# Mixer group 0 in a fixed TensorE order: chunk scan and gate columns placed by hand instead of by the scheduler

## The chip, the cores and the metric

The kernel runs on one core of one Trainium2 chip. The metric is the device time of one execution in microseconds (us). Before the change it is 1347.84 us, the median of 3 runs (1347.83 to 1347.86).

## The reference

A two-layer decoder trunk over 512 tokens of width 1024, all in float32. Layer 0 is a Mamba-2 mixer and a convolutional feed-forward block; layer 1 is differential attention on shared keys and values and another such block. Only the mixer matters here:

```python
zxbcdt = rms_norm(x, ln_g) @ in_w                      # z (gate), x, B, C, dt
xbc = silu(causal_dwconv(xbc, conv_w, conv_b))
y = ssd_chunked(xs32 * dt, a, bm, cm)                  # 4 groups of 8 heads, 4 chunks of 128 tokens
    cb     = einsum('bclgn,bcsgn->bcgls', cc, bc)
    y_diag = einsum('bcgls,bgrcls,bcsgrp->bclgrp', cb, decay_in, xc)
    states = einsum('bclgn,bgrcl,bclgrp->bcgrpn', bc, decay_states, xc)   # carried from chunk to chunk
    y_off  = einsum('bclgn,bcgrpn,bgrcl->bclgrp', cc, states_in, exp(a_cs))
y = (y + xs32 * d_skip) * silu(z)
return rms_norm(y, per group) @ out_w
```

## The kernel before, in words

**Tiling.** The stream lies feature-major as eight tiles of 128 features by 512 tokens, each split into a high part `xgh` and a low part `xgl`. A weight block of 1024 by 128 columns is fetched by SyncE (SP) into a raw tile `wr`, split by ScalarE into `wh` (line 147) and by VectorE into `wl` (line 151), and multiplied in three passes per 128 features (lines 197, 198, 199): 24 matmuls of 128x512 per block, called **wide** below. Blocks are named after their column block: `in32` and `in36` are B and C of group 0, `in16` to `in19` its x, `in0` to `in3` its gate z; `in33`, `in37`, `in20` to `in23` the same of group 1.

**Groups and chunks.** The mixer goes over four groups. `conv_block` makes B, C and the four x blocks of a group: VectorE scales the product by the token norm (line 532, `u`), ScalarE starts the convolution (line 535, `ctmp`), VectorE adds three taps (line 537), ScalarE applies SiLU (line 539). Then the scan runs over four chunks of 128 tokens, called a, b, c and d in the code (`c0` to `c3` of a tile's number), while the gate columns fill TensorE.

**The steps of a chunk.** `turned` transposes B (tile `bt`). `decays` masks the decay matrix `m` on GpSimd (line 635) and takes eight exponentials on ScalarE (line 640). `masked` computes `cb` (line 646) and multiplies `m` by it on VectorE (line 647). `tokens` transposes x (`xs`, line 655) and weights it twice on VectorE (`xe`, `xd`, lines 658 and 660). `states` computes the chunk's state (`st`, line 685) and adds it to the one before (`S`). `preceding` applies the state before it (`yo`, line 676; VectorE, line 678). `products` are sixteen small matmuls (`y`, line 699 before and 701 after the change), and `outputs` adds them to x on VectorE (lines 708 and 711 before, 710 and 713 after). After the scan the group's x is gated (line 831), squared (`gsq`, line 833), summed (`gacc`, line 838), transposed to token norms (`tr_g`, line 448), taken to the power -1/2 by a chain of tiny VectorE steps ending in line 251, and spread back along the tokens by TensorE (`al_g`, line 458).

**What sets the order.** A scheduler places each engine's instructions at build time; within an engine they then run in that order. In groups 1 to 3 `woven` switches the scheduler off for TensorE (`manual_schedule`): after each of the 32 steps of `z_steps` (three wide matmuls each) a table `at` says which chunk steps come. Group 0 is left to the scheduler: `weave(scan(cs), z_blocks(g, zs), 2, 3)` offers the chunk steps in order and two gate blocks for every three of them. `tc.issue_after(x)` holds the placing of what follows until `x` has been placed. Small products share a ring of four banks of the matmul accumulator (`aux_bank`), so a small matmul also waits until the reader of an earlier one in its bank is done.

**Function tables.** Exponentials and SiLU lie in different tables of ScalarE; a change between them shows in the trace as ACT_TABLE_LOAD.

Of the kernel before, what the change touches and what calls it, by code (L numbers as in the profile page):

```python
# [18 lines left out]
P = 128  # L19
T = 512  # L20
D = 1024
KB = D // P
NT = T // P
# [3 lines left out]
HPG = 8  # L27
# [12 lines left out]
def trunk_kernel(ctx: ExitStack, tc, x, ssm_ln_g, ssm_in_w, ssm_conv_w, ssm_conv_b, ssm_dt_bias,  # L40
# [4 lines left out]
    act, dve, pool, pe, sync = nc.scalar, nc.vector, nc.gpsimd, nc.tensor, nc.sync  # L45
# [11 lines left out]
    def mm_bank(name):  # L57
        return pp.tile([P, T], F32, tag="mm", name=name)
# [129 lines left out]
    def chunk(key):  # L188
        while state["next"] <= state["use"] + AHEAD and state["next"] < len(plan):
            emit_chunk()  # L190
        state["use"] += 1
        k, h, l = ready.pop(0)
        assert k == key, (k, key)
        return h, l
# [59 lines left out]
    with tc.tile_pool(name="ph0", bufs=1) as p0:  # L254
# [24 lines left out]
        ps = aux_bank("pst")  # L279
# [193 lines left out]
    def weave(main, fill, num, den):  # L473

        owed = 0
        for _ in main:
            owed += num
            while owed >= den:
                owed -= den
                next(fill, None)  # L480
        run(fill)
# [37 lines left out]
    with tc.tile_pool(name="ssm_y", bufs=1) as yp, tc.tile_pool(name="ssm", bufs=1) as sp:  # L519
        def in_block(key):  # L520
            wh, wl = chunk(key)
            if key in ("in32", "in36"):
                return ps_b0 if key == "in32" else ps_b1
            ps = mm_bank("ps_" + key)
            for k in range(KB):
                state["last"] = mm3(ps, wh[:, k, :], wl[:, k, :], xgh[k], xgl[k], k == 0, k == KB - 1)
            return ps
# [81 lines left out]
        class Chunk:  # L609
# [22 lines left out]
            def decays(self):  # L632


                pool.affine_select(out=self.m, in_=self.m, pattern=[[0, HPG], [1, P]], compare_op=ALU.is_ge,
                                   fill=NEG, base=0, channel_multiplier=-1)
                for h in range(HPG):
                    v = self.m[:, 4 * (h % 2) + h // 2, :]
                    col = self.hh.start + h
                    act.activation(v, v, AF.Exp, bias=ncum[:, col:col + 1])  # L640

            def masked(self):

                cs = self.cs
                ps = aux_bank("cb" + self.tag)
                pe.matmul(ps[:, :P], self.bT[:, cs], self.cT[:, cs], start=True, stop=True)
                dve.tensor_tensor(out=self.m, in0=self.m, in1=ps[:, :P].unsqueeze(1).to_broadcast([P, HPG, P]),
                                  op=ALU.mult)

            def tokens(self):  # L650

# [28 lines left out]
            def states(self):  # L680

                tag, c = self.tag, self.c
                if c < NT - 1:
                    ps = aux_bank("st" + tag)
                    pe.matmul(ps, self.bt, fl(self.xe), start=True, stop=True)
                    self.S = sp.tile([P, HPG, 64], F32, tag="S", name="S" + tag, bufs=2)
                    if c == 0:
                        act.activation(fl(self.S), ps, AF.Copy)
                    else:
                        dve.tensor_tensor(out=self.S, in0=self.prev.S, in1=self.per_head(et), op=ALU.mult)  # L690
                        dve.tensor_tensor(out=self.S, in0=byh(ps), in1=self.S, op=ALU.add)

            def products(self):

# [27 lines left out]
                    add_to_stream(m, ps, 16, norm)  # L722
                    yield

        def z_blocks(g, zs):
            for b in range(4):
                ps = in_block("in%d" % (4 * g + b))
                z = sp.tile([P, T], F32, tag="z", name="z%d_%d" % (g, b), bufs=4)
                dve.tensor_tensor(out=z, in0=ps, in1=rr[0], op=ALU.mult)
                act.activation(z, z, AF.Silu)  # L730
                zs.append(z)
                yield

        def z_steps(g, zs):
            for b in range(4):
                wh, wl = chunk("in%d" % (4 * g + b))
                ps = mm_bank("ps_in%d" % (4 * g + b))
                for k in range(KB):
                    state["last"] = mm3(ps, wh[:, k, :], wl[:, k, :], xgh[k], xgl[k], k == 0, k == KB - 1)
                    if k == KB - 1:  # L740
                        z = sp.tile([P, T], F32, tag="z", name="z%d_%d" % (g, b), bufs=4)
                        dve.tensor_tensor(out=z, in0=ps, in1=rr[0], op=ALU.mult)
                        act.activation(z, z, AF.Silu)
                        zs.append(z)
                    yield

# [3 lines left out]
                cs.append(Chunk(g, c, bT, cT, xs, cs[-1] if cs else None))  # L750
            return cs

        def scan(cs):
            for t in range(NT + 1):
                if t < NT:
                    cs[t].tokens()
                    if t < NT - 1:
                        cs[t].turned()
                    cs[t].masked()
                if t == 0:  # L760
                    cs[2].decays()
                    cs[3].decays()
                if t:
                    cs[t - 1].preceding()
                    cs[t - 1].states()
                    cs[t - 1].products()
                    cs[t - 1].outputs()
                yield

        def woven(cs, g, zs):  # L770

            def pair(a, b):
                a.products()
                b.products()
                a.outputs()
                b.outputs()

            a, b, c, d = cs
            at = {0: (a.turned, b.turned, c.decays), 1: (a.masked, b.masked, d.decays),
                  10: (a.tokens,), 11: (b.tokens,), 13: (a.states,), 15: (b.preceding, b.states),  # L780
                  16: (lambda: pair(a, b), c.turned, c.masked), 18: (c.tokens,), 19: (c.preceding, d.tokens),
                  20: (d.masked,), 21: (c.states,), 24: (d.preceding,), 25: (lambda: pair(c, d),)}
            with tc.manual_schedule(engines={mybir.EngineType.PE}):
                behind = 5 if g == 1 else 0
                for n, _ in enumerate(z_steps(g, zs)):
                    for f in at.get(n - behind, ()):
                        f()

# [17 lines left out]
        for g in range(NG):  # L806
            bT = sp.tile([P, T], F32, tag="bT", name="bT%d" % g, bufs=2)
            cT = sp.tile([P, T], F32, tag="cT", name="cT%d" % g, bufs=2)
            xs_ = sp.tile([P, 4, T], F32, tag="xs", name="xs%d" % g, bufs=2)
            cs = chunks(g, bT, cT, xs_)  # L810
            for c in cs:
                c.fetch()
            conv_block(16 + g, "in%d" % (32 + g), bT)
            if g:
                prev = normed(*todo)
            conv_block(20 + g, "in%d" % (36 + g), cT)
            if g == 0:
                params_a()
            xs = [xs_[:, b, :] for b in range(4)]
            for b in range(4):  # L820
                if b >= 2:
                    cs[b - 2].decays()
                conv_block(4 * g + b, "in%d" % (16 + 4 * g + b), xs[b])
            zs = []
            if g:
                woven(cs, g, zs)
            else:
                weave(scan(cs), z_blocks(g, zs), 2, 3)
            acc = None
            for b in range(4):  # L830
                dve.tensor_tensor(out=xs[b], in0=xs[b], in1=zs[b], op=ALU.mult)
                sq = sp.tile([P, T], F32, tag="gsq", name="gsq%d_%d" % (g, b), bufs=2)
                act.activation(sq, xs[b], AF.Square)
                if b == 0:
                    acc = sq
                else:
                    a2 = sp.tile([P, T], F32, tag="gacc", name="gacc%d_%d" % (g, b), bufs=2)
                    (pool if b == 1 and g else dve).tensor_tensor(out=a2, in0=acc, in1=sq, op=ALU.add)
                    acc = a2
            factor = lambda: token_rsqrt(acc, sp, "g%d" % g, 512)  # L840
            if g == 0:
                params_b()
                todo = g, xs, factor()
            elif g < NG - 1:
                run(out_proj(g - 1, *prev, None))
                todo = g, xs, factor()
            else:
                op = out_proj(g - 1, *prev, None)
                for _ in range(3):
                    next(op)  # L850
                rt = factor()
                for _ in range(2):
                    next(op)
                prev = normed(g, xs, rt)
                run(op)
# [486 lines left out]
```

## Time and profile before

| What | us |
|---|---|
| median of 3 runs | 1347.84 |
| the profiled execution | 1347.89 |
| its span from the first to the last instruction | 1346.2 |
| TensorE (PE) busy in the span | 1340.2 |
| VectorE (DVE), ScalarE (ACT), GpSimd (POOL) busy | 913.8, 644.1, 105.0 |
| group 0's gate blocks, chunks, and blocks in33 and in37 | 50.88 to 98.09 |

The profiled execution is 0.05 us above the median, so a sum made against it can be carried to the median with that difference. The span leaves out 1.7 us that lie around it. A row of the timeline gives start, duration, engine, line, operation, tiles and count, and at the end in brackets how long the engine had been idle and what released it. Matmuls overlap, so the cost of one in a row of them is the distance from its start to the next start, not its printed duration. The chain of work that ended last lists pieces with just that cost.

### The profile page before, as it was taken

Reading aid. Unit: us, or ns where it says so; the run is one execution under the profiler, and the core shown is the slowest. Engines: PE = TensorE matmul, PEld = TensorE weight load, DVE = VectorE, ACT = ScalarE, POOL = GpSimd, SP = SyncE. Lnnn points to the kernel's source line nnn. Section 1 sums busy time; section 2 is a strip of 40 time slices with the busy share of each in tenths; the row PEclk is TensorE's granted clock in tenths of the full one; section 3 lists DMA queues with packets and bytes.
Section 4 is the critical chain, followed back from the end, with each engine's and each line's share of the span. In section 5 each row is a group of like instructions: output and inputs, shape, how many; then the busy total and the mean of one; then the engine's idle time right before and its main releaser. Section 6 shows DMA issues by size and latency. Waiting matters only on the chain.

```text
span 1346.2 us, 16887 instructions
## 1 busy us (share of the span) xinstructions
PE 1340.2 (100%) x6423; PEld 1097.1 (81%) x6423; DVE 913.8 (68%) x1527; ACT 644.1 (48%) x1058; POOL 105.0 (8%) x141
## 2 busy tenths in 40 slices
PE   9999999999999999999999999999999999999998
PEld 7878888888888888888888887777888888888887
DVE  5989788788877774367754556778777773367743
ACT  6696553652444442234433556777654442134420
POOL 6330401200110000000002200000100000000000
PEclk9999999999999999999999999999999999999999
DMA  7543533432333332333323422221233322333322
GB/s 205 160 150 94 145 98 111 132 94 71 94 94 94 97 107 94 94 94 95 101 79 105 131 79 93 69 81 50 64 94 94 94 94 95 95 105 97 94 94 78
DMA packets 179825, 134.98 MB, mean 100 GB/s; under 512 B 6492, under 2 KB 163552, under 8 KB 179744
## 3 DMA queue, kind: packets, MB, share of 16 engines
q1 hardware_dynamic: 173872, 120.73, 29.6%
q0 software_dynamic: 4592, 12.08, 3.0%
q8 instruction: 50, 0.82, 0.3%
q10 hardware_dynamic: 1280, 1.10, 0.2%
q14 instruction: 31, 0.25, 0.1%
HBM read 131.64 MB, written 2.25 MB: 99 GB/s over the span
## 4 chain that ended last, share of the span: by engine, by line
PE 97%; DVE 1%; ACT 1%; DMA 0%; issue 0%; SPq 0%
PE ps_g L198 6%; PE ps_u L199 6%; PE ps_g L199 6%; PE ps_u L197 6%; PE ps_u L198 6%; PE ps_g L197 6%; PE ps_in L197 5%; PE ps_in L199 5%; PE ps_in L198 5%; PE ps_d L198 3%; PE ps_d L199 3%; PE ps_d L197 3%; PE ps_d L923 3%; PE ps_d L921 3%; PE ps_d L922 3%; PE ps_o L198 2%
## 5 line engine op out<-in xcount | busy, mean ns | idle before, releaser
L197 PE MATMUL ps_u<-xgh,wh_u 128*128 128x512 f32 x352 | 137.4, 390 | 0.0
L198 PE MATMUL ps_g<-xgl,wh_g 128*128 128x512 f32 x352 | 137.1, 389 | 0.0
L197 PE MATMUL ps_g<-xgh,wh_g 128*128 128x512 f32 x352 | 137.0, 389 | 0.0
L199 PE MATMUL ps_u<-xgh,wl_u 128*128 128x512 f32 x352 | 137.0, 389 | 0.0
L199 PE MATMUL ps_g<-xgh,wl_g 128*128 128x512 f32 x352 | 137.0, 389 | 0.0
L198 PE MATMUL ps_u<-xgl,wh_u 128*128 128x512 f32 x352 | 136.9, 389 | 0.0
L197 PE MATMUL ps_in<-xgh,wh_in 128*128 128x512 f32 x304 | 126.0, 414 | 0.0
L151 DVE TENSOR_TENSOR wl_d<-wr_d,wh_d 128x1024 fp32r<-128x1024 f32 (+1 forms) x46 | 54.2, 1179 | 96.9 <-ACT wh_d L147 96.7
L199 PE MATMUL ps_in<-xgh,wl_in 128*128 128x512 f32 x304 | 119.8, 394 | 0.0
L198 PE MATMUL ps_in<-xgl,wh_in 128*128 128x512 f32 x304 | 119.2, 392 | 0.0
L147 ACT ACTIVATE wh_d<-wr_d 128x1024 fp32r<-128x1024 f32 (+1 forms) x46 | 47.1, 1024 | 130.6 <-PE ps_d L923 58.0
L882 DVE TENSOR_TENSOR uu<-ps_u,nr_f 128x512 f32<-128x512 f32 x44 | 30.4, 691 | 77.6 <-PE ps_u L199 77.6
L953 ACT ACTIVATE hh<-vg 128x512 fp32r<-128x512 f32 x44 | 27.8, 632 | 114.9 <-DVE vg L952 114.9
L198 PEld LDWEIGHTS ps_g<-xgl,wh_g 128*128 128x128 f32 x352 | 66.1, 188 | 14.0 <-DVE xgl L430 0.3
L199 PEld LDWEIGHTS ps_u<-xgh,wl_u 128*128 128x128 f32 x352 | 66.1, 188 | 13.7
L197 PEld LDWEIGHTS ps_g<-xgh,wh_g 128*128 128x128 f32 x352 | 66.1, 188 | 13.7
L199 PEld LDWEIGHTS ps_g<-xgh,wl_g 128*128 128x128 f32 x352 | 66.1, 188 | 13.7
L198 PEld LDWEIGHTS ps_u<-xgl,wh_u 128*128 128x128 f32 x352 | 66.1, 188 | 13.6
L197 PEld LDWEIGHTS ps_u<-xgh,wh_u 128*128 128x128 f32 x352 | 66.1, 188 | 13.5
L147 ACT ACTIVATE wh_g<-wr_g 128x1024 fp32r<-128x1024 f32 x44 | 46.7, 1061 | 50.3 <-PE ps_u L198 30.9
L197 PE MATMUL ps_d<-hh,wh_d 128*128 128x512 f32 x176 | 68.5, 389 | 0.0
L198 PE MATMUL ps_d<-hl,wh_d 128*128 128x512 f32 x176 | 68.5, 389 | 0.0
(361 smaller groups left out, 3175.1 us busy)
## 6 DMA issues: line engine op xcount, KB each, us to landing
wr_g<-in_ffn_up_w_dram SPq DMA_DIRECT2D x44, 512.0 KB, 3.7
wr_u<-in_ffn_up_w_dram SPq DMA_DIRECT2D x44, 512.0 KB, 3.7
wr_d<-in_ffn_down_w_dram SPq DMA_DIRECT2D x42, 512.0 KB, 3.6
wr_in<-in_ssm_in_w_dram SPq DMA_DIRECT2D x40, 512.0 KB, 3.8
m<-cumd POOLq DMA_DIRECT2D x16, 512.0 KB, 4.7
wr_out<-in_ssm_out_w_dram SPq DMA_DIRECT2D x16, 512.0 KB, 3.3
wr_k<-in_kv_w_dram SPq DMA_DIRECT2D x8, 512.0 KB, 3.7
wr_q<-in_q_w_dram SPq DMA_DIRECT2D x8, 512.0 KB, 3.7
```

Of the source, the lines that this page charges most:

```text
L147: return act.activation(self.wh[:, :self.n], self.raw[:, :self.n], AF.Copy)
L151: return eng.tensor_tensor(out=self.wl[:, :self.n], in0=self.raw[:, :self.n], in1=self.wh[:, :self.n].bitcast(F32), op=ALU.subtract)
L197: pe.matmul(ps, wh, xh, start=start, stop=False)
L198: pe.matmul(ps, wh, xl, start=False, stop=False)
L199: return pe.matmul(ps, wl, xh, start=False, stop=stop).ins
L882: dve.tensor_tensor(out=u, in0=ps, in1=r, op=ALU.mult)
L921: pe.matmul(pss[b], hh[k][:, ts], wh[:, k - k0, :], start=k == 0, stop=False)
L922: pe.matmul(pss[b], hh[k][:, ts], wl[:, k - k0, :], start=False, stop=False)
L923: pe.matmul(pss[b], hl[k][:, ts], wh[:, k - k0, :], start=False, stop=k == stop)
L953: act.activation(h, ga, AF.Copy)
```

## The change

Group 0 now goes through `woven` too, with a table of its own; the scheduler no longer places its TensorE work. Against the table of the other groups, the exponentials of all four chunks stand at step 7, `cb` of chunks a and b stands behind the state of chunk a, `cb` of the third chunk one step behind the pair of products, and the end of the scan is spread to step 31. Four more edits belong to it: chunk b's `preceding` and `states` are placed after the weighing of its `m` (`taken_up`), the outputs of chunk a on VectorE after chunk b's new state (`behind`), the second gate block's SiLU after the exponentials of chunk d, and the weights fetched ahead at the third gate block after the exponentials of chunk b. The first state of group 0 is copied out by VectorE (line 688) instead of ScalarE.

```diff
                     self.S = sp.tile([P, HPG, 64], F32, tag="S", name="S" + tag, bufs=2)
-                    if c == 0:
+                    if c == 0 and self.g == 0:
+                        dve.tensor_copy(fl(self.S), ps)
+                    elif c == 0:
                         act.activation(fl(self.S), ps, AF.Copy)
                     else:
                         dve.tensor_tensor(out=self.S, in0=self.prev.S, in1=self.per_head(et), op=ALU.mult)
-                        dve.tensor_tensor(out=self.S, in0=byh(ps), in1=self.S, op=ALU.add)
+                        self.summed = dve.tensor_tensor(out=self.S, in0=byh(ps), in1=self.S, op=ALU.add).ins
...
-        def z_steps(g, zs):
+        def z_steps(g, zs, cs):
             for b in range(4):
-                wh, wl = chunk("in%d" % (4 * g + b))
+                key = "in%d" % (4 * g + b)
+                if g == 0 and b == 2:
+                    with tc.issue_after(cs[1].decayed):
+                        wh, wl = chunk(key)
+                else:
+                    wh, wl = chunk(key)
...
-                        act.activation(z, z, AF.Silu)
+                        if g == 0 and b == 1:
+                            with tc.issue_after(cs[3].decayed):
+                                act.activation(z, z, AF.Silu)
+                        else:
+                            act.activation(z, z, AF.Silu)
...
-            def pair(a, b):
+            def pair(a, b, behind=None):
                 a.products()
                 b.products()
-                a.outputs()
+                with tc.issue_after(behind) if behind is not None else nullcontext():
+                    a.outputs()
                 b.outputs()
 
+            def taken_up(c):
+                with tc.issue_after(c.weighed):
+                    c.preceding()
+                    c.states()
...
+            if g == 0:
+                at = {0: (a.turned, b.turned), 7: (a.decays, b.decays, c.decays, d.decays),
...
+                      17: (lambda: taken_up(b),), 20: (lambda: pair(a, b, b.summed), c.turned), 21: (c.masked,),
...
             for b in range(4):
-                if b >= 2:
+                if g and b >= 2:
                     cs[b - 2].decays()
                 conv_block(4 * g + b, "in%d" % (16 + 4 * g + b), xs[b])
             zs = []
-            if g:
-                woven(cs, g, zs)
-            else:
-                weave(scan(cs), z_blocks(g, zs), 2, 3)
+            woven(cs, g, zs)
```

What this makes of the engines' orders shows at three places. On TensorE before, the end of the scan stands inside the last gate block `in3` (tile `ps_in3`): transposes, `cb`, `yo`, one wide matmul, a state and the products of chunk c follow each other.

```order
L655 MATMUL xs0_3_839<-ident_77,xs0_429 128x128 x4
L646 MATMUL cb0_3_846<-cT0_428,bT0_427 128x128
L676 MATMUL yo0_2_849<-cT0_428,S0_1_788 128x128 x4
L198 MATMUL ps_in3_934<-xgl5_99,wh_in3_807 128x512
L685 MATMUL st0_2_855<-xe0_2_769,bt0_2_775 128x512
L699 MATMUL y0_2_860<-m0_2_437,xd0_2_771 64x128 x8
L199 MATMUL ps_in3_934<-xgh5_91,wl_in3_808 128x512
```

After, `cb` of chunk c, the transposes of c and the pieces behind them stand between whole steps of three wide matmuls, in the third gate block `in2` and the fourth.

```order
L646 MATMUL cb0_2_854<-cT0_428,bT0_427 128x128
L197 MATMUL ps_in2_793<-xgh6_92,wh_in2_641 128x512
L198 MATMUL ps_in2_793<-xgl6_100,wh_in2_641 128x512
L199 MATMUL ps_in2_793<-xgh6_92,wl_in2_642 128x512
L655 MATMUL xs0_2_860<-ident_77,xs0_429 128x128 x4
L197 MATMUL ps_in2_793<-xgh7_93,wh_in2_641 128x512
L198 MATMUL ps_in2_793<-xgl7_101,wh_in2_641 128x512
L199 MATMUL ps_in2_793<-xgh7_93,wl_in2_642 128x512
L676 MATMUL yo0_2_875<-cT0_428,S0_1_808 128x128 x4
L655 MATMUL xs0_3_881<-ident_77,xs0_429 128x128 x4
```

So the pieces moved one gate block earlier and no longer follow each other directly, except `yo` and the transposes behind it. On VectorE after, one step of chunk b's outputs stands ahead of chunk b's new state (`S_1`, line 693), the outputs of chunk a and the rest of chunk b's behind it, and then the weighing of chunk c's `m`.

```order
L678 TENSOR_TENSOR er_1_434<-yo_1_800,er_1_434 128x512
L692 TENSOR_TENSOR S_1_808<-S_0_773,dec 128x512
L710 TENSOR_SCALAR xs_429<-xs_429,c_103,y_1_829 128x128
L693 TENSOR_TENSOR S_1_808<-st_1_806,S_1_808 128x512
L710 TENSOR_SCALAR xs_429<-xs_429,c_103,y_0_820 128x128 x4
L710 TENSOR_SCALAR xs_429<-xs_429,c_103,y_1_829 128x128 x3
L647 TENSOR_TENSOR m_2_437<-m_2_437,cb_2_854 128x1024
```

Before, chunk a's outputs stood ahead of chunk b's state. On ScalarE after, at the start of group 1 (blocks `in23` and `in4`), exponentials of group 1's last chunk alternate with SiLU and convolution steps, so table loads stand between them.

```order
L418 ACTIVATE le<-le 128x2
L147 ACTIVATE wh_in_1187<-wr_in_1185 128x1024
L640 ACTIVATE m_3_1038<-m_3_1038,ncum 128x128
L539 ACT_TABLE_LOAD
L539 ACTIVATE cT_1024<-ctmp_1140 128x512
L535 ACTIVATE ctmp_1179<-u_1177,c_102 128x512
```

Before, that exponential stood ahead of the load that `bT` needs, and no load stood between `wh_in23` and `ctmp` of the next block.

More of the change, by code (lines that the diff above doesn't have):

```diff
@@ L639, in decays @@
                     col = self.hh.start + h
-                    act.activation(v, v, AF.Exp, bias=ncum[:, col:col + 1])
+                    self.decayed = act.activation(v, v, AF.Exp, bias=ncum[:, col:col + 1]).ins
             def masked(self):
@@ L646, in masked @@
                 pe.matmul(ps[:, :P], self.bT[:, cs], self.cT[:, cs], start=True, stop=True)
-                dve.tensor_tensor(out=self.m, in0=self.m, in1=ps[:, :P].unsqueeze(1).to_broadcast([P, HPG, P]),
-                                  op=ALU.mult)
+                self.weighed = dve.tensor_tensor(
+                    out=self.m, in0=self.m, in1=ps[:, :P].unsqueeze(1).to_broadcast([P, HPG, P]), op=ALU.mult).ins
             def tokens(self):
@@ L723, in out_proj @@
                     yield
-        def z_blocks(g, zs):
+        def z_steps(g, zs, cs):
             for b in range(4):
-                ps = in_block("in%d" % (4 * g + b))
-                z = sp.tile([P, T], F32, tag="z", name="z%d_%d" % (g, b), bufs=4)
-                dve.tensor_tensor(out=z, in0=ps, in1=rr[0], op=ALU.mult)
-                act.activation(z, z, AF.Silu)
-                zs.append(z)
-                yield
-        def z_steps(g, zs):
-            for b in range(4):
-                wh, wl = chunk("in%d" % (4 * g + b))
-                ps = mm_bank("ps_in%d" % (4 * g + b))
+                key = "in%d" % (4 * g + b)
[4 more added lines that the diff above has]
+                    wh, wl = chunk(key)
+                ps = mm_bank("ps_" + key)
                 for k in range(KB):
@@ L742, in z_steps @@
                         dve.tensor_tensor(out=z, in0=ps, in1=rr[0], op=ALU.mult)
-                        act.activation(z, z, AF.Silu)
+                        if g == 0 and b == 1:
[3 more added lines that the diff above has]
+                            act.activation(z, z, AF.Silu)
                         zs.append(z)
@@ L751, in chunks @@
             return cs
[L753 to L768, printed above, removed]
@@ L770, in woven @@
         def woven(cs, g, zs):
-            def pair(a, b):
+            def pair(a, b, behind=None):
                 a.products()
                 b.products()
-                a.outputs()
+                with tc.issue_after(behind) if behind is not None else nullcontext():
+                    a.outputs()
                 b.outputs()
+            def taken_up(c):
+                with tc.issue_after(c.weighed):
+                    c.preceding()
+                    c.states()
             a, b, c, d = cs
[L779 to L782, printed above, removed]
+            if g == 0:
+                at = {0: (a.turned, b.turned), 7: (a.decays, b.decays, c.decays, d.decays),
+                      11: (a.tokens,), 12: (b.tokens,), 14: (a.states,), 15: (a.masked, b.masked),
+                      17: (lambda: taken_up(b),), 20: (lambda: pair(a, b, b.summed), c.turned), 21: (c.masked,),
+                      22: (c.tokens,), 23: (c.preceding, d.tokens), 24: (d.masked,), 26: (c.states,),
+                      30: (d.preceding,), 31: (lambda: pair(c, d),)}
+            else:
+                at = {0: (a.turned, b.turned, c.decays), 1: (a.masked, b.masked, d.decays),
+                      10: (a.tokens,), 11: (b.tokens,), 13: (a.states,), 15: (b.preceding, b.states),
+                      16: (lambda: pair(a, b), c.turned, c.masked), 18: (c.tokens,), 19: (c.preceding, d.tokens),
+                      20: (d.masked,), 21: (c.states,), 24: (d.preceding,), 25: (lambda: pair(c, d),)}
@@ L783, in woven @@
             with tc.manual_schedule(engines={mybir.EngineType.PE}):
                 behind = 5 if g == 1 else 0
-                for n, _ in enumerate(z_steps(g, zs)):
+                for n, _ in enumerate(z_steps(g, zs, cs)):
                     for f in at.get(n - behind, ()):
```

## The prediction

> **What bounds the kernel now.** I read the page first: its totals and the shares of the chain that ended last.
>
> ```profile
> span 1346.2 us, 16887 instructions
> PE 1340.2 (100%) x6423; PEld 1097.1 (81%) x6423; DVE 913.8 (68%) x1527; ACT 644.1 (48%) x1058; POOL 105.0 (8%) x141
> PE 97%; DVE 1%; ACT 1%; DMA 0%; issue 0%; SPq 0%
> ```
>
> TensorE is busy for 1340.2 of 1346.2 us and carries 97% of the chain. The end moves only by what TensorE's stream gets shorter or by what it is made to wait. A busy TensorE can still lose time between matmuls, so I took the stretch that the change rewrites: from the first matmul of `in0` to the first of `in20`. It holds the same work before and after.
>
> ```profile
> 50.88:98.09 47.21, 47.16 (x273) 37.19 (x272) 38.42 (x67) 38.59 (x88) 22.09 (x28) 1.00 0.60 182
> ```
>
> The columns are the stretch's length, then the busy time of PE, PEld, DVE, ACT and POOL, then the granted clock, DMA share and GB/s. TensorE works through all 47.21 us at clock 1.00, with DVE and ACT at four fifths. Next the timeline, for the price of a wide matmul and for what lies around the products.
>
> ```profile
> 61.62 0.39 PE L197 MATMUL ps_in<-xgh,wh_in 128*128 128x512 f32 x1
> ...
> 71.38 0.39 PE L198 MATMUL ps_in<-xgl,wh_in 128*128 128x512 f32 x1
> 71.82 1.09 PE L699 MATMUL y<-m,xd 128*64 128x128 f32 x16
> 72.85 0.66 PE L655 MATMUL xs<-ident,xs 128*128 128x128 f32 x4
> ...
> 80.92 1.02 PE L685 MATMUL st<-xe,bt 128*128 128x512 f32 x2
> 81.87 1.09 PE L699 MATMUL y<-m,xd 128*64 128x128 f32 x16
> ```
>
> From 61.62 to 71.38 lie 43 starts, 0.227 us each. Six blocks of 24 make 144 wide matmuls or 32.69 us, so the chunk work costs 47.21 - 32.69 = 14.5 us now. That is all the change can touch directly. Part is loss: the products at 71.82 come 0.44 us after a wide start where 0.227 would do, and those at 81.87 come 0.95 us after their state.
>
> **What the fixed order costs on TensorE.** Groups 1 to 3 run such an order already, so the chain has the price of each piece, the slow restart of the wide stream behind it included. Columns: start, cost, piece.
>
> ```profile
> 125.97 0.44 PE cb L646 x4
> 132.58 0.44 PE xs L655 x4
> 135.55 0.86 PE st L685 x2
> 137.80 0.89 PE yo L676 x8
> 138.69 0.86 PE st L685 x2
> 140.26 1.90 PE y L699 x32
> 142.16 0.26 PE bt L666
> 87.86 0.30 PE pst L236 x2
> ```
>
> With the new order's pieces in turn: the first transposes with `ps_cum`, `pst` and two `bt`, about 0.55 in two pieces (estimated from the two transposes of parameters, 0.30, and one `bt`, 0.26); two `xs` 0.88; `st` 0.86; two `cb` 0.44; `yo` and `st` 1.75; two products and `bt` 1.90 + 0.10 lead-in + 0.23; single `cb` 0.23; `xs` 0.44; `yo` and `xs` 1.33; `cb` 0.23; `st` 0.86; `yo` 0.89; two products with two `pst` 2.25; two `pst` 0.28. That is 13.2 us: 1.3 us less than 14.5 if TensorE never waits. I take 1.2, since some of these prices are read to 0.03 us only.
>
> **The waits it adds.** First, `ps_cum` stands two wide matmuls earlier (at 51.56 on the clock of before) and needs the copy of `cum`.
>
> ```profile
> 51.32 0.28 DVE L596 COPY cum<-ps_dec 128x128 f32<-128x128 f32 x1
> 52.01 0.27 PE L602 MATMUL ps_cum<-ident,cum 128*128 128x128 f32 x1
> ```
>
> The copy ends at 51.60; with the hand-over TensorE waits about 0.15 us.
>
> Second, the third chunk's `cb` takes the bank of chunk b's state, so it waits for VectorE's addition (line 693). VectorE has put one step of chunk b's outputs ahead of that addition, and this step waits for the end of chunk b's products.
>
> ```profile
> 77.92 0.69 DVE L691 TENSOR_TENSOR S<-st,S 128x512 f32<-128x512 f32 x1
> 79.19 1.12 DVE L708 SCALAR_TENSOR_TENSOR xs<-xs,c,y 128x128 f32<-128x128 f32 x4 [0.58 <-PE y L699]
> 80.23 0.68 DVE L660 TENSOR_TENSOR xd<-xs,dt 128x512 f32<-128x512 f32 x1
> ...
> 78.05 1.09 PE L699 MATMUL y<-m,xd 128*64 128x128 f32 x16
> 79.08 0.66 PE L655 MATMUL xs<-ident,xs 128*128 128x128 f32 x4
> ```
>
> Outputs start 0.11 us after TensorE has gone on (79.08 to 79.19) and cost 0.26 each (79.19 to 80.23, four). So the addition ends 0.11 + 0.26 + 0.69 = 1.06 us after, about 1.15 with the hand-over. TensorE meanwhile has `bt` (0.14 to the next start) and three wide matmuls with a slow restart (0.77), 0.91 us. Wait: 0.25 us. Behind it the third chunk's transposes need the bank of chunk a's products, that is four more outputs: the addition's slot of 0.60 and 4 x 0.26, done at about 2.2; TensorE arrives at 2.1. Wait: 0.10 us. Queued behind both on TensorE is everything, so they count in full. The other chunk steps have cover: the first state, whose copy the change moves to VectorE (taken as one line 660 step, 0.60), is multiplied at 62.7 and copied by about 64.2, and `yo` of chunk b, behind 54 wide matmuls and 2.9 us of pieces, comes at 66.0. Were that 1.8 us of cover gone, TensorE would wait for the rest.
>
> Third, the exponentials. They must be done before the products of chunks a and b. TensorE reaches those behind 63 wide matmuls (14.3 us) and 4.6 us of pieces, at 69.8, chunk b's 1.0 later.
>
> ```profile
> 61.58 6.70 POOL L635 TENSOR_SCALAR_AFFINE_SELECT m<-m 128x1024 f32<-128x1024 f32 x4
> 66.60 1.28 ACT L640 ACT_TABLE_LOAD   x1
> 67.90 9.48 ACT L640 ACTIVATE m<-m,ncum 128x128 f32<-128x128 f32 x32
> ```
>
> GpSimd's masks do not move; the first ends near 63.2 (6.70 / 4 behind 61.58). ScalarE before starts its exponentials only at 67.90, behind two SiLUs. After, one SiLU and a load stand ahead and it starts at 63.3. Chunk b's are done 16 x 0.296 = 4.7 us later at 68.0, its weighing (1.2 us) at 69.3. TensorE wants it at 70.8. No wait, 1.5 us of cover.
>
> **What is late next.** ScalarE changes table ten times instead of six between 58 and 109 us, and the group norm hangs on it.
>
> ```profile
> 96.94 1.14 ACT L833 ACTIVATE gsq<-xs 128x512 f32<-128x512 f32 x2
> 97.98 0.80 ACT L535 ACTIVATE ctmp<-u,c 128x512 f32<-128x512 f32 x1
> 98.68 1.05 ACT L147 ACTIVATE wh_in<-wr_in 128x1024 fp32r<-128x1024 f32 x1
> 99.63 0.80 ACT L535 ACTIVATE ctmp<-u,c 128x512 f32<-128x512 f32 x1
> ...
> 103.18 1.28 ACT L539 ACT_TABLE_LOAD   x1
> 104.47 0.63 ACT L539 ACTIVATE bT<-ctmp 128x512 f32<-128x512 f32 x1
> 98.91 0.68 DVE L838 TENSOR_TENSOR gacc<-gacc,gsq 128x512 f32<-128x512 f32 x1
> 99.92 0.60 PE L448 MATMUL tr_g<-ident,gacc 128*128 128x128 f32 x4
> 110.82 0.60 PE L458 MATMUL al_g<-ident,tr_g 128*128 128x128 f32 x4
> ```
>
> If `in20` starts 0.7 us earlier, at 97.4, `tr_g` behind 18 of its wide matmuls (8 before) is reached at 97.4 + 4.1 = 101.5. VectorE's sum `gacc` was done at 99.6 before; adding VectorE's steps in the new order from the end of `in33` (ten of 0.60, one split of about 1.1, three taps of about 0.7) I get 101.4. A tie. `al_g` behind 4 wide matmuls of `in22` is reached at 97.4 + 48 x 0.227 + 0.44 + 4 x 0.227 = 109.65. Ahead of the last step of line 251 on VectorE now stands a tap of block `in20`, which needs ScalarE's start of that block. ScalarE is free for `wh_in22` when TensorE has read `in37`, at 97.5, and then has two splits of 0.95, two squares 1.04, two starts (0.71 and 0.80), five exponentials 1.5, three loads with what follows at 1.29 each 3.9, two SiLUs of 0.54, and 0.4 of small steps: 11.3 us, to 108.8. With the tap and line 251 the norm is there at 109.7. I take a wait of 0.1 us there; each later ScalarE step counts in full.
>
> Two views of a table change differ. In the row, the next instruction starts 1.29 us after a load of 1.28 (103.18 to 104.47). The Trainium skill (ScalarE: Activation LUTs, What ACT_TABLE_LOAD costs) adds to a load of about 1283 ns a drain of about 1380 ns, 2.66 us per change; the trace agrees with the load and shows no drain. By it the three changes would put ScalarE 3 x 1.38 = 4.1 us later, an estimate from that page.
>
> **Sum.** 1.2 us less work, 0.15 + 0.25 + 0.10 + 0.10 = 0.6 us of waits: 0.6 us gained. 1347.89 - 0.6 = 1347.3 for the profiled execution, 1347.25 for the median, which lies 0.05 below it; I say 1347.3. Beyond 110 us the orders converge and TensorE has no wait to win back. Bounds: no waits at all gives 1346.6 and is the low end. At the high end one more step the size of a load (1.29) late at `al_g` gives 1348.6.
>
> **The rivals.** *Full gain* (0.12): the ties fall well and VectorE is quicker; 1347.84 - 1.2 = 1346.6. For it: the same pieces in group 1 show no wait. Against: the wait for line 693 is built into the order.
>
> *ScalarE late at the norm* (0.16), the one on the other side: from the point at which ScalarE's start of `in20` comes more than 0.6 us after 108.8, `al_g` eats the gain. The masks of group 1's third chunk are the likely cause, since their fetch now waits for products that come about 5 us later; one load's worth gives 1347.3 + 1.3 = 1348.6. For it: both norm steps tie in my sum. Against: nothing in ScalarE's rows shows a reserve spent.
>
> *A table change costs a second load's time* (0.02): three times 1.28 at `al_g`, 1347.3 + 3.8 = 1351.1. Against: the rows above. The drain in the Trainium skill's page is such a price.
>
> *Nothing moves* (0.05): VectorE's waits grow to the whole 1.2; 1347.84.
>
> The forecast keeps 0.65: 1346.9 to 1347.8. The range 1346.6 to 1348.6 leaves out the double load and part of the tails. I call a difference over 0.2%, 2.7 us, faster or slower, about what a measurement of this kernel can tell from no change. The stretch cannot give 2.7 us, so faster gets 0.02. Slower needs 3.3 us of waits: 0.04. Within: 0.94.
>
> **What would show it.** Right: `in20` starts near 97.4 instead of 98.09; `cb` of chunk c stands about 0.25 us behind its wide neighbour; exponentials from about 63.3 to 72.8; `al_g` near 109.8. Wrong: `in20` at or after 98.09 (my prices or waits), a start of `tr_g` or `al_g` more than 0.7 us behind its neighbour (the ScalarE rival), products that wait for the weighing, or any difference that lies after 130 us.

## The result, and the profile after

The changed kernel takes 1350.13 us (median of 20 runs, 1349.20 to 1350.95) against 1347.99 us (median of 20 runs, 1347.66 to 1348.48) for the kernel before: 2.1 us slower, a ratio of 1.0016 with a 95% interval of 1.0010 to 1.0022. That is under the 0.2% that I had set as the bound for slower, and outside the predicted range of 1346.6 to 1348.6. The profiled execution of the changed kernel took 1350.06 us. From its page, the totals and the shares of the chain that ended last:

```profile
span 1348.4 us, 16893 instructions
PE 1340.5 (99%) x6423; PEld 1097.3 (81%) x6423; DVE 915.6 (68%) x1528; ACT 651.3 (48%) x1063; POOL 103.6 (8%) x141
PE 95%; DVE 1%; ACT 1%; DMA 1%; issue 0%; POOL 0%; SPq 0%; POOLq 0%
```

The same work on TensorE, now 2.2 us longer: TensorE waits. The stretch from `in0` to `in20`, and the waits of TensorE from 45 to 125 us (total, times, longest):

```profile
50.66:97.83 47.17, 46.87 (x274) 37.14 (x272) 38.45 (x66) 40.05 (x86) 19.39 (x27) 1.00 0.64 183
```

```profile
PE tr_g L448 <- DVE s2t L415: 1.8, 1, 1.8
PE cb L646 <- DVE S L693: 0.2, 1, 0.2
PE al_g L458 <- DVE tr_g L251: 0.2, 1, 0.2
```

The stretch lasts 47.17 us instead of 47.21: of the 0.7 us that I expected there, 0.04 is left. The loss lies behind it, on TensorE's timeline of the changed kernel:

```profile
97.83 0.39 PE L197 MATMUL ps_in<-xgh,wh_in 128*128 128x512 f32 x1
...
101.68 0.39 PE L199 MATMUL ps_in<-xgh,wl_in 128*128 128x512 f32 x1
103.90 0.63 PE L448 MATMUL tr_g<-ident,gacc 128*128 128x128 f32 x4 [1.83 <-DVE s2t L415]
...
111.89 0.39 PE L197 MATMUL ps_in<-xgh,wh_in 128*128 128x512 f32 x1
112.43 0.65 PE L458 MATMUL al_g<-ident,tr_g 128*128 128x128 f32 x4 [0.15 <-DVE tr_g L251]
...
127.01 0.38 PE L666 MATMUL bt<-ident,bT 128*128 128x128 f32 x2
```

and of the kernel before, the same `bt`, group 1's first:

```profile
124.89 0.38 PE L666 MATMUL bt<-ident,bT 128*128 128x128 f32 x2
```

`tr_g` stands 2.22 us behind its neighbour where 0.23 would be no wait, `al_g` 0.54. That is 2.0 and 0.3 us more than without a wait, and `in20` starts 0.26 us earlier than before, so these two make the whole loss; from `bt` on, the two kernels run alike, 2.1 us apart. (The page names L415 as the releaser of `tr_g`, the tiny step right behind the sum `gacc` on VectorE; `tr_g` reads the sum.) So the question is why the sum came at 103.75 and not at 101.4. VectorE of the changed kernel from the end of `in33` to the sum (line 713 is the last addition of the outputs, 826 the gating, 833 the sum `gacc`):

```profile
92.59 0.69 DVE L532 TENSOR_TENSOR u<-ps_in,nr_x 128x512 f32<-128x512 f32 x1 [0.68 <-PE ps_in L199]
93.19 1.56 DVE L713 TENSOR_TENSOR xs<-xs,er 128x512 f32<-128x512 f32 x1
94.68 1.21 DVE L151 TENSOR_TENSOR wl_in<-wr_in,wh_in 128x1024 fp32r<-128x1024 f32 x1
95.82 2.49 DVE L826 TENSOR_TENSOR xs<-xs,z 128x512 f32<-128x512 f32 x4
98.23 0.68 DVE L833 TENSOR_TENSOR gacc<-gsq,gsq 128x512 f32<-128x512 f32 x1
98.83 1.57 DVE L537 SCALAR_TENSOR_TENSOR ctmp<-u,c,ctmp 128x511 f32<-128x511 f32 x1
100.32 0.68 DVE L532 TENSOR_TENSOR u<-ps_in,nr_x 128x512 f32<-128x512 f32 x1
100.92 0.73 DVE L537 SCALAR_TENSOR_TENSOR ctmp<-u,c,ctmp 128x510 f32<-128x510 f32 x1
101.80 0.69 DVE L833 TENSOR_TENSOR gacc<-gacc,gsq 128x512 f32<-128x512 f32 x1
102.41 0.74 DVE L537 SCALAR_TENSOR_TENSOR ctmp<-u,c,ctmp 128x509 f32<-128x509 f32 x1
103.07 0.68 DVE L833 TENSOR_TENSOR gacc<-gacc,gsq 128x512 f32<-128x512 f32 x1
```

GpSimd beside it (line 625 asks for the fetch of a matrix `m`, line 635 masks it; these are chunks c and d of group 1):

```profile
88.69 0.56 POOL L625 DMA_DIRECT2D m<-cumd  x1 [7.83 <-PE y L701]
89.55 0.54 POOL L625 DMA_DIRECT2D m<-cumd  x1 [0.30 <-PE pst L236]
...
93.13 1.09 POOL L635 TENSOR_SCALAR_AFFINE_SELECT m<-m 128x1024 f32<-128x1024 f32 x1 [0.64 <-DMA m<-cumd]
...
98.24 1.61 POOL L635 TENSOR_SCALAR_AFFINE_SELECT m<-m 128x1024 f32<-128x1024 f32 x1 [2.14 <-DMA m<-cumd]
```

Both fetches write tiles that the products of group 0's chunks c and d must have read. The changed kernel makes these products as one pair at 87.04 and asks for both fetches within 0.9 us; the kernel before asked at 83.51 and 88.94, and masked at 87.90 and 93.46. ScalarE (line 640 the exponentials, 828 the squares):

```profile
99.89 0.40 ACT L640 ACTIVATE m<-m,ncum 128x128 f32<-128x128 f32 x1 [1.32 <-POOL m L635]
100.20 1.05 ACT L147 ACTIVATE wh_in<-wr_in 128x1024 fp32r<-128x1024 f32 x1
101.15 1.14 ACT L828 ACTIVATE gsq<-xs 128x512 f32<-128x512 f32 x2
```

Two readings fit these rows. **S**: ScalarE. It waits 1.32 us for the second mask, whose fetch took 8.6 us, with an exponential that stands ahead of the split and of the last two squares. This is the chain of waits that the profile prints for 90 to 106 us: fetch, mask, split, squares. **V**: VectorE. Between 92.59 and 103.75 it idles for 0.2 us only; line 713 and the first tap of line 537 take 1.56 and 1.57 us, where 0.68 and 0.74 are their normal durations, and each lies beside a mask. A third theory, **B**, is that the two chains nearly tie, so that mending one uncovers the other.

### The profile page after: what moved, and what is told of

It reads as the page before. It is cut to its first block, busy times and chain, and to the rows that moved or that the text cites. A ratio compares the mean times of both kernels' runs of the same rounds, so it can differ in the third digit from the quotient of the medians.

```text
span 1348.4 us, 16893 instructions
## 1 busy us (share of the span) xinstructions
PE 1340.5 (99%) x6423; PEld 1097.3 (81%) x6423; DVE 915.6 (68%) x1528; ACT 651.3 (48%) x1063; POOL 103.6 (8%) x141
## 4 chain that ended last, share of the span: by engine, by line
PE 95%; DVE 1%; ACT 1%; DMA 1%; issue 0%; POOL 0%; SPq 0%; POOLq 0%
PE ps_g L198 6%; PE ps_u L197 6%; PE ps_u L198 6%; PE ps_g L197 6%; PE ps_u L199 6%; PE ps_g L199 6%; PE ps_in L197 5%; PE ps_in L198 5%; PE ps_in L199 5%; PE ps_d L197 3%; PE ps_d L198 3%; PE ps_d L199 3%; PE ps_d L916 3%; PE ps_d L917 3%; PE ps_d L918 3%; PE ps_o L197 2%
## 5 line engine op out<-in xcount | busy, mean ns | idle before, releaser
L199 PEld LDWEIGHTS ps_g<-xgh,wl_g 128*128 128x128 f32 x352 | 66.2, 188 | 13.8
L198 PEld LDWEIGHTS ps_u<-xgl,wh_u 128*128 128x128 f32 x352 | 66.2, 188 | 13.4
```

Source lines behind the costliest of these rows:

```text
L198: pe.matmul(ps, wh, xl, start=False, stop=False)
L199: return pe.matmul(ps, wl, xh, start=False, stop=stop).ins
```

## The experiments

All differences are to the kernel before, run beside each kernel on the same chip. "The sum's row" is the time on VectorE from the start of line 532 for `in33` to the end of `gacc`: 11.16 us in the changed kernel. The 95% interval of each ratio reaches about 0.1%, 1.2 us, to either side, so runs less than that apart are not told apart by their medians; the readings rest on the traces, one execution of each kernel.

**Only ScalarE mended.** `state["sq"]` is the last square.

```diff
-  self.decayed = act.activation(v, v, AF.Exp, ...).ins
+  with tc.issue_after(state["sq"]) if (self.g, self.c) == (1, 3) else nullcontext():
+      self.decayed = act.activation(v, v, AF.Exp, ...).ins
```

> On ScalarE the exponentials of m1_3 (group 1's fourth chunk) are placed behind the last square gsq0_3; nothing else of the change is undone. Theory S (the chain that the profile prints: fetch of m1_3, mask, its first exponential, split of in22, squares): ScalarE is free at 98.6 instead of 100.2, the squares end 1.6 us earlier and tr_g waits 0.2 instead of 1.8: about 1348.4. Theory V (VectorE's own row from in33's end to gacc sets the time): VectorE has only 0.21 us of idle time ahead of gacc2, so at most that: 1349.9. Theory B (the two chains nearly tie): 0.2 us as well, 1349.9, and VectorE's row has no idle time left ahead of gacc3.

1349.38 us, 1.3 above the kernel before (ratio 1.0009, 1.0000 to 1.0019). The squares were done at 100.8, a microsecond and a half earlier, and VectorE had no idle time left from 93.0 to 103.2; TensorE still waited, and not for ScalarE:

```profile
PE tr_g L448 <- DVE s2t L415: 0.8, 1, 0.8
```

By S only 0.2 us of this wait would be left. The sum's row took 10.18 us, 1.0 less rather than 0.2, because in this run the second mask met other VectorE steps (it came at 99.68, its fetch took 9.7 us).

**Only VectorE relieved.** The taps of `in33` and `in37` and the split of `in22` behind the sum (`state["ga"]`):

```diff
-  dve.scalar_tensor_tensor(out=tmp[:, s:], ...)
+  with tc.issue_after(state["ga"]) if j in (17, 21) else nullcontext():
+      dve.scalar_tensor_tensor(out=tmp[:, s:], ...)
```

> On VectorE the taps of in33 and in37 and the split of in22 are placed behind the sum gacc0_3, so that about 2.8 us of steps leave VectorE's row ahead of the sum; ScalarE's order ahead of the squares stays. S: the third and fourth square still end at 101.7 and 102.2, VectorE is not the limit, nothing gained: 1350.1. V: the sum is done near 101 and the whole wait of 1.8 goes: 1348.3. B: the sum follows the squares, two sums of 0.6 from 101.8, done near 103.0 instead of 103.75: 0.75 gained, 1349.4. In all three al_g can come later, since the taps stand in its way now, by up to 0.5.

1350.79 us (1349.11 to 1352.37), 2.7 above; the trace is of an execution of 1349.44. Of the steps held, only the three taps of `in33` (2.0 us) had stood ahead of the sum, and the two masks still lengthened two steps there. The sum's row took 9.84 us. VectorE of this run now waits for ScalarE's third square:

```profile
101.19 1.49 DVE L833 TENSOR_TENSOR gacc<-gacc,gsq 128x512 f32<-128x512 f32 x2 [0.80 <-ACT gsq L828]
```

**Both.**

> Both holds of the two runs beside it. S: as with the exponential alone, 1348.4. V: as with the taps alone, 1348.3. B: only here does the whole wait at tr_g go, 1348.3, against 1349.9 and 1349.4 for the single holds. al_g can again come up to 0.5 later.

1348.93 us, 0.9 above (1.0006, 0.9997 to 1.0015): the sum's row fell to 9.1 us. It took 10.2 with the first hold and 9.8 with the second: either engine alone keeps the sum late, as B says. The scheduler had put `tr_g` four and five wide matmuls earlier in the last two runs, so TensorE still waited 0.9 us there; only the row's length can be compared.

**Without the masks.** Chunks c and d of group 1 leave out the mask and the decay (`act.activation(v, v, AF.Exp, scale=0.0)`).

> Chunks c and d of group 1 leave out GpSimd's mask (line 635) and their exponentials leave out the decay (they give 1), with as many exponentials as before; all fetches stay. If GpSimd's masks stretch VectorE's steps beside them, line 713 at 93.2 and the first tap of in33 take 0.7 each instead of 1.56 and 1.57, and the exponential of m1_3 no longer stands behind a mask: V and B give 1.6 to 1.7 us, 1348.4. S: ScalarE's exponential starts at the landing, 98.2 instead of 99.9: also 1.6, but with VectorE's two steps unchanged at 1.56. If the masks are not the reason, VectorE's steps stay long and the sum comes at 103.5: 1349.9.

1349.13 us, 1.1 above. VectorE of this run:

```profile
93.33 0.68 DVE L713 TENSOR_TENSOR xs<-xs,er 128x512 f32<-128x512 f32 x1
...
98.08 0.74 DVE L537 SCALAR_TENSOR_TENSOR ctmp<-u,c,ctmp 128x511 f32<-128x511 f32 x1
...
101.12 0.69 DVE L833 TENSOR_TENSOR gacc<-gacc,gsq 128x512 f32<-128x512 f32 x1 [1.04 <-ACT gsq L828]
```

The two long steps are back at 0.68 and 0.74: the masks had stretched them. The sum is late all the same, now for ScalarE, whose exponentials wait for a fetch of 8.8 us. The row took 10.36 us. Undisturbed it takes 9.21, as the next run shows: of the 2.0 us lost, 1.2 stay here through ScalarE alone, and 1.0 stayed through VectorE with ScalarE mended. Either alone holds at least half of the delay.

**Masks and exponentials out of the way of both engines.** A tiny GpSimd step that reads the finished norm stands ahead of the two masks:

```diff
+  state["pl"] = pool.tensor_tensor(out=hold, in0=r, in1=r, op=ALU.add).ins     # r: norm of group 0
...
+  with tc.issue_after(state["pl"]) if self.g == 1 and self.c in (2, 3) else nullcontext():
       pool.affine_select(out=self.m, ...)
```

> GpSimd masks chunks c and d of group 1 only after the norm of group 0 (line 251) is done, through a tiny GpSimd step that reads it; the exponentials behind the masks go late with them. TensorE's order is unchanged, VectorE's up to al_g too. Theory B (masks stretch two VectorE steps by 0.85 each, and the exponentials hold ScalarE's squares): VectorE's row from in33's end to the sum loses 1.7 us and its 0.2 us of waiting, the sum is done near 101.8 where TensorE arrives at 101.9: the wait of 1.8 at tr_g and the 0.3 at al_g go, 1348.1. Rival: the late exponentials (4.7 us on ScalarE) come back as a wait for al_g's readers or for the products of group 1, a difference that lies after 110 us: 1349 to 1350.

The first and the last step of the sum's row on VectorE, then TensorE of this run at the norm, and its waits:

```profile
92.85 0.69 DVE L532 TENSOR_TENSOR u<-ps_in,nr_x 128x512 f32<-128x512 f32 x1 [0.69 <-PE ps_in L199]
...
101.38 0.68 DVE L833 TENSOR_TENSOR gacc<-gacc,gsq 128x512 f32<-128x512 f32 x1
```

```profile
101.95 0.39 PE L199 MATMUL ps_in<-xgh,wl_in 128*128 128x512 f32 x1
102.21 0.63 PE L448 MATMUL tr_g<-ident,gacc 128*128 128x128 f32 x4
```

```profile
PE xs L655 <- ACT xs L539: 1.3, 1, 1.3
PE cb L646 <- DVE S L693: 0.2, 1, 0.2
```

With VectorE's order unchanged, the sum's row took 9.21 us; `tr_g` stands 0.26 us behind its neighbour and `al_g` 0.23. The whole loss at the norm is gone, and group 1's first `bt` starts at 124.95 instead of 127.01. Yet the time is 1349.68 us, 1.8 above: the rival of this run came true as well. The 16 exponentials, pushed late, now stand on ScalarE ahead of a SiLU (line 539), and the transposes of group 1 wait for it.

**The two fetches apart.** Chunk c's products at step 27 instead of beside chunk d's:

```diff
-  30: (d.preceding,), 31: (lambda: pair(c, d),)}
+  27: (c.products, c.outputs), 30: (d.preceding,), 31: (d.products, d.outputs)}
```

> Products and outputs of chunk c come at step 27 instead of in a pair with chunk d's at step 31, so the fetch of m1_2 is asked for about 4 us earlier and that of m1_3 no longer shares the memory with it. If the two fetches side by side make the 8.6 us: that of m1_3 lands in 4.5 to 6 us, its mask and exponential come before ScalarE is free for the split of in22, one mask leaves VectorE's row: 1.0 to 1.6 us gained at tr_g, 0.4 paid for one more break in the wide stream: 1349.2. If the weight fetch of 512 KB beside it makes the length: 8 us still, 1350.3.

1348.75 us, 0.9 above (1.0008, 0.9999 to 1.0016). The two fetches from issue to landing in the changed kernel, and then in this run:

```profile
DMA to landing us min/median/max: 4.4/6.5/8.6
```

```profile
DMA to landing us min/median/max: 4.6/4.8/4.9
```

Asked for at 83.06 and 89.82 us, neither takes over 5 us. In the changed kernel both are asked for within 0.9 us, and a 512 KB fetch of weights in the same microsecond; here the weights' fetch too comes later, so this run shows that the crowd makes the 8.6 us, not which of its members. (In the run with `cb` back, below, the pair stays and the weights are asked for 2.6 us behind it; the second fetch takes 6.4 us there. Both members seem to count.) `tr_g` does not wait. The scheduler also reordered VectorE and ScalarE, so the gain cannot be split between the fetch and the new order.

**Outputs of chunk a no longer held** (`pair(a, b)` instead of `pair(a, b, b.summed)`).

> The outputs of chunk a are no longer held behind the addition of chunk b's state; only VectorE's order changes, by one step: ahead of the addition stands an output of chunk a instead of one of chunk b, whose products end 1 us earlier. The wait of cb of the third chunk for line 693, 0.46 us more than its price, goes. If VectorE's row to the sum starts with in33's end and so moves with TensorE: 0.45 gained, 1349.7. If the row hangs on the fetch and on work before: TensorE only waits longer at tr_g, 1350.1.

1349.25 us, 1.4 above, against 2.1 for the changed kernel; the trace is of an execution of 1348.54. `cb` costs 0.24 us instead of 0.69 and the state at 79 us 0.88 instead of 1.07; the sum's row starts 0.66 us earlier with TensorE and ends 1.0 earlier, and `tr_g` still stands 1.84 us behind its neighbour. The hold had put an output of chunk b, whose products end last, ahead of the addition that `cb` waits for.

**Late masks and unheld outputs.**

> The late masks and the unheld outputs together: with the wait at tr_g gone, TensorE keeps the 0.45 us of the cb: 1347.7, which would be 0.3 below the kernel before. If the sum is now just what TensorE waits for, the 0.45 comes back as a wait at tr_g: 1348.1.

1348.90 us, 1.0 above. Group 1's first `bt` starts at 124.02, 0.87 us ahead of the kernel before, and then the transposes lose it:

```profile
131.52 0.49 PE L655 MATMUL xs<-ident,xs 128*128 128x128 f32 x3
133.33 0.33 PE L655 MATMUL xs<-ident,xs 128*128 128x128 f32 x1 [1.31 <-ACT xs L539]
```

**What a mask costs through VectorE alone.** Two runs with the exponentials of chunks c and d of group 1 behind that SiLU, so that ScalarE is free for the squares in both, and outputs unheld in both; the first with late masks, the second with masks as in the changed kernel.

> As the late masks with unheld outputs, and the exponentials of chunks c and d of group 1 stand on ScalarE behind the last SiLU of group 1's x (line 539). The wait of 1.54 us for that SiLU at the transposes of group 1 (133.3 in the run before) should go and nothing else should wait: 1348.9 - 1.5 = 1347.4, below the kernel before by 0.5. If the 16 exponentials (4.7 us and three table loads) then come too late for the weighing of group 1's chunks c and d (their cb at 143 and 148), TensorE waits there instead: 1348.5 or more.

> As the run beside it, but GpSimd masks as early as in the changed kernel: only the exponentials are late. ScalarE is free for the squares, so the difference to the run beside it is what the masks alone cost through VectorE. If a mask holds a VectorE step that reads two tiles in place (0.6 to 0.9 us for each of two masks): the sum comes 1.2 to 1.7 us later, TensorE waits 1.0 to 1.6 at tr_g, 1348.6. If the masks cost only through ScalarE's exponentials: no wait at tr_g, 1347.4 as beside it.

TensorE of the first:

```profile
101.18 0.39 PE L199 MATMUL ps_in<-xgh,wl_in 128*128 128x512 f32 x1
101.44 0.63 PE L448 MATMUL tr_g<-ident,gacc 128*128 128x128 f32 x4
...
139.67 1.91 PE L676 MATMUL yo<-cT,S 128*128 128x128 f32 x8 [2.64 <-ACT S L690]
```

VectorE and TensorE of the second:

```profile
92.59 1.36 DVE L713 TENSOR_TENSOR xs<-xs,er 128x512 f32<-128x512 f32 x1
...
97.42 1.58 DVE L833 TENSOR_TENSOR gacc<-gsq,gsq 128x512 f32<-128x512 f32 x1
...
102.93 0.63 PE L448 MATMUL tr_g<-ident,gacc 128*128 128x128 f32 x4 [1.45 <-DVE s2t L415]
```

`tr_g` 0.26 us behind its neighbour with late masks, 1.84 with early ones, everything else ahead of it in the same order: the masks alone cost 1.58 us, through VectorE. As times both runs are bad (1351.55 and 1352.54 us, 3.6 and 4.6 above): the exponentials now stand ahead of the copy of group 1's first state (line 690), and `yo` waits 2.6 and 2.0 us for it. My expectation of 1347.4 had looked only one reader ahead.

**`cb` of the third chunk back at step 20.**

> The changed kernel with cb of the third chunk back at step 20, right behind the products, as in the other groups; the scheduler then also puts the first two squares ahead of the exponentials of m1_2. cb waits for line 693 with 0.68 us less of wide matmuls ahead of it: about 1.1 us of wait where it is 0.46 now. If VectorE's row to the sum moves with TensorE: 0.6 more, 1350.7; with ScalarE's squares earlier up to 0.2 of it comes back.

1349.30 us, 1.3 above; 0.8 below the changed kernel, where I expected 0.6 worse. `cb` waited 0.9 us as expected, but the scheduler, given the other order, put the first two squares ahead of the exponentials, and this saved more at `tr_g` (1.11 us behind its neighbour). In this trace one place of one `cb` is worth less than what it stirs up on the engines that the table does not fix.

**A better version.** Late masks, unheld outputs, and the 16 exponentials behind the copy of group 1's first state: their `decays` are moved in group 1's table from steps 0 and 1 to the step of `a.states` and held behind line 690.

> As the late masks with unheld outputs, but the exponentials of chunks c and d of group 1 stand on ScalarE behind the copy of group 1's first state (line 690), so that neither the SiLU of x (1.54 us lost at 133) nor that copy (2.6 to 2.8 us lost at 137 in the run with the exponentials behind the SiLU) has them ahead. If those were the only late readers, TensorE keeps what it had at 124 (0.87 us ahead of the kernel before): 1347.1, faster than both kernels. If 16 exponentials and a load (6.1 us from about 136 to 142) now come too late for the weighing behind cb at 143 and 147 or hold the split of the output weights behind them: a new wait of 1 us or more, 1348.2 or above.

1347.44 us (1347.11 to 1347.97, 11 runs) against 1348.04 (1347.74 to 1348.39, 14 runs): 0.6 below the kernel before and 2.7 below the changed one. The ratio to the kernel before is 0.9996 with an interval of 0.9986 to 1.0005, so that it beats the kernel before is likely, not settled. Between 45 us and the end, the view of waits shows none for TensorE.

## Why the prediction was wrong, point by point

**The step that failed: "A tie" at `tr_g`.** I summed VectorE's row from the end of `in33` (ten steps of 0.60, one of 1.1, three of 0.7, 9.2 us) and got 101.4. The row takes 9.21 us when no mask lies beside it (late masks). In the changed kernel it takes 11.16: 0.88 and 0.83 for the two steps beside masks, 0.2 of waiting for ScalarE's third square; and it began at 92.59, 0.4 later than I had it. I knew where the masks would come, and named their late fetch in a rival, but looked for the price on ScalarE and at `al_g`. I gave every VectorE step its undisturbed duration and GpSimd's work none on VectorE. The trace of before held the warning on the other engine: one of its masks, at 93.46, took 1.54 us instead of 1.09, beside a gating step of VectorE:

```profile
93.36 0.69 DVE L831 TENSOR_TENSOR xs<-xs,z 128x512 f32<-128x512 f32 x1 [0.18 <-ACT z L730]
93.46 1.54 POOL L635 TENSOR_SCALAR_AFFINE_SELECT m<-m 128x1024 f32<-128x1024 f32 x1 [1.90 <-DMA m<-cumd]
```

**The waits in the stretch: 0.5 us predicted, 1.1 measured.** The first transposes with `ps_cum` cost 0.96 us against 0.55 without a wait (I had 0.15 of wait; 0.4 came), `cb` 0.69 against 0.23 (0.25; 0.46 came), the transposes of chunk c 0.51 against 0.44 (0.10; 0.07 came), and a state 1.07 against 0.86, which I had not foreseen. The mechanism of the second was right: with the outputs unheld the wait is gone. **The work was right**: in that run's order the pieces sum to 13.8 us, 13.4 without the wait of `ps_cum`, against my 13.2.

**`al_g`: 0.1 us predicted, 0.3 measured.** It was a consequence: with `tr_g` on time it stands 0.23 us behind its neighbour. Together 0.6 us more in the stretch, 2.0 at `tr_g` and 0.2 here are the 2.8 us between the forecast and the result.

**Right**: exponentials from 63.3 to 72.8 (62.63 to 72.28 in the trace), products of both pairs without a wait for the weighing, no difference behind 130 us. `in20` started at 97.83 rather than 97.4, and most of its lead over the kernel before (98.09) is older than the change: the changed kernel's trace runs 0.22 us ahead at 50 us already.

**The rivals.** ScalarE late at the norm pointed to the right source, the masks of group 1 behind a late fetch, with about half the price (1.3 instead of the 2.3 lost at both steps), with one of the two engines and the wrong place. A double price of a table change is excluded: ScalarE's load at 103.88 takes 1.28 us and the SiLU behind it starts at 105.18. The drain that the Trainium skill (ScalarE: Activation LUTs, What ACT_TABLE_LOAD costs) adds does not show here either. My sum also left no room for what a late step meets: `tr_g` and `al_g` were both ties by my own working, and a tie of two sums of ten steps is not worth 0.65 of certainty.

## What to carry to other kernels

Where a sum of durations ends in a tie, look for what else runs beside each of its steps, on the other engines too: a row of undisturbed durations is a lower bound. An engine with idle time (GpSimd, 8% busy) can still cost the busy ones time, by when its work falls. When a step is pushed out of the way, follow its whole queue: the exponentials held up the squares, then the SiLU, then the copy of a state, and only in their fourth place did TensorE show no wait.

## What the runs showed of the hardware

**In these traces a GpSimd mask and a VectorE step that reads two tiles hold each other up.** Line 713 (`xs`, `er`), the taps (`u`, `ctmp`) and `gacc` (two squares) take 0.68 to 0.74 us alone and up to 1.6 beside a mask; started second, the mask takes 1.61 (98.24, beside a `gacc`) and 2.15 us, beside the split below, instead of 1.09. A VectorE step that takes one of its operands from TensorE's accumulator (`ps_in`) is not touched. GpSimd and VectorE of the changed kernel, one pair of each kind:

```profile
64.08 1.09 POOL L635 TENSOR_SCALAR_AFFINE_SELECT m<-m 128x1024 f32<-128x1024 f32 x1 [0.45 <-DMA m<-cumd]
```

```profile
64.53 0.69 DVE L740 TENSOR_TENSOR z<-ps_in,nr_x 128x512 f32<-128x512 f32 x1
```

```profile
77.67 1.21 DVE L151 TENSOR_TENSOR wl_in<-wr_in,wh_in 128x1024 fp32r<-128x1024 f32 x1
77.69 2.15 POOL L635 TENSOR_SCALAR_AFFINE_SELECT m<-m 128x1024 f32<-128x1024 f32 x1 [1.08 <-DMA m<-cumd]
```

The Trainium skill (SBUF — State Buffer, SBUF: two separate sides) describes an exclusive lock on a port that both engines share: whichever starts first holds it for its whole instruction, and a VectorE instruction with two inputs there takes part. The trace agrees in both directions: with the mask first, 93.13 + 1.09 is 94.22, and line 713, started at 93.19, ends 0.53 us after that; with the split first, the mask at 77.69 ends 0.96 us after the split.

**Two fetches of 512 KB side by side.** With the weights' fetch asked for in the same microsecond, the second of the pair took 7.8 to 9.7 us in the profiled runs; with the weights 2.6 us behind the pair 6.4; and 4.9 when it was asked for 6.8 us behind the first.

**Open:** the executions of the changed kernel spread over 1.75 us, those of the kernel before over 0.8 beside it (in another series one of 31 lay 1.6 us above the rest), those of the last version over 0.9. The changing length of this fetch is a candidate, but the first run with exponentials behind the SiLU, which kept the masks away from the norm, spread over 1.9 us too; no run tested it by itself.
